# First block of a two-block transformer: low parts of weights on VectorE in the head norms and branches, head copies on ScalarE, wider rotation, six early gate units

## Chip, cores and metric

The kernel runs on one core of one Trainium2 chip. The metric is the device time of one execution in microseconds (us), the median of several runs. A core has TensorE (PE, matrix products; PEld is its weight load), VectorE (DVE), ScalarE (ACT), GpSimd (POOL) and SyncE (SP), whose queue issues the weight transfers here. Each engine runs its own queue in order.

## The reference, cut to what matters

256 tokens of width 1024 pass a first block and then two layers of a second block. Only the first block is touched. What it computes:

```python
h = rmsnorm(x, mix_norm_g)
proj = h @ w_in                       # 1024 x 5632
qa, ka, va, qd, kd, vd, qm, graw = split(proj)   # 3x384, 3x384, 256, 3x1024 columns
qa = rope(rmsnorm(heads(qa)), positions)         # 6 heads of 64; ka, qd, kd alike
qm = rmsnorm(heads(qm))                          # 4 heads
mkv = rmsnorm(mem) @ w_mem_kv                    # 1024 x 512
o_a = moba_attention(qa, ka, va) @ w_branch_moba
o_d = dilated_attention(qd, kd, vd) @ w_branch_dil
o_m = memory_attention(qm, rmsnorm(mk), mv) @ w_branch_mem
g = sigmoid(graw)                                # three gates of 1024 columns
x = x + (g0 * o_a + g1 * o_d + g2 * o_m) @ w_out
# then a feed-forward part with a convolution over three tokens, then the second block
```

All of it is in float32, which sets how the weights are handled.

## The kernel before, in words

**Split weights.** A weight slab of 128 rows is loaded by `wload` (L88) into `raw`; ScalarE rounds it into `hi` (L102) and another engine subtracts, `lw = raw - hi` (L103). The product is then three matmuls: `hi` and `lw` against the high part of the activations (L184, L185), `hi` against their low part (L187). Which engine makes `lw` follows a pattern set by `lo_on`: `lo_on(V, GP)` takes VectorE and GpSimd in turn, `lo_on(GP)` GpSimd alone. `raw` has four buffers, `hi` and `lw` three each, so the parts of a slab are made two to three slabs ahead of their use.

**Units.** `gemm_n` (L189) goes over the slabs of a product; with 1024 columns a slab is one unit of 12 matmuls of 128x512 (four accumulators in PSUM, of which there are four in all), with 512 columns six matmuls.

**Order of the first block.** The projection runs over column groups of 1024, 1024 and 512 (L363), then the memory projection of 512 columns (L371, eight units). Meanwhile VectorE and ScalarE run the head norms (`head_norm`, L407) and the rotation (`rope_pair`, L423) on the finished columns `pj`. `head_T` (L439) transposes q and k on TensorE and copies them into `qkT`, the middle group of three on VectorE (L451), the others on ScalarE (L449). The 24 gate units (3 gates by 8 slabs) are a list `fill`: `some_fill(2)` (L484) takes two ahead of the first `head_T`, `run_pairs` (L284) takes one after each of 16 attention steps, and what is left (six) runs at L508. The attention (L212) forms scores (L221), their maximum on VectorE (L236), the exponential on ScalarE (L243), transposes (L262), and the product with v (L275). Then come three branch products of 3, 3 and 2 slabs (L512); VectorE multiplies each by its gate (L518) and adds it to `merged` (L521, eight adds of 128x512). `merged` is transposed (L529) and multiplied by `w_out` (L533).

**What sets the order.** The kernel is written as straight code; a planner orders each engine's instructions by the place in the code (earlier is preferred) and by when it estimates operands and buffers to be ready. On the chip that order is fixed: an engine whose next instruction has to wait holds up everything behind it.

**GpSimd's part before.** In the memory projection every second `lw` is GpSimd's (L347, `lo_on(V, GP)`); from L481, `lo_on(GP)`, all 24 gate units, the 8 branch slabs and the 8 slabs of `w_out` are GpSimd's. From L537 on the two engines take turns again.

Of the kernel before, what the change touches and what calls it, by code (L numbers as in the profile page):

```python
# [10 lines left out]
F32 = mybir.dt.float32  # L11
# [39 lines left out]
def moba_peer_stack_kernel(ctx: ExitStack, tc: tile.TileContext, A, out):  # L51
    nc = tc.nc
    V, SC, GP, PE, SY = nc.vector, nc.scalar, nc.gpsimd, nc.tensor, nc.sync
# [14 lines left out]
    def tmp_tile():  # L68
        tmp = ptmp.tile([128, 512], F32)
        return tmp  # L70
# [7 lines left out]
    def P(name, i=None):  # L78
        o, w = PV[name]
        return pv[:, o:o + w] if i is None else pv[:, o + i:o + i + 1]  # L80
# [4 lines left out]
    def lo_on(*pat):  # L85
        pol["pat"], pol["i"] = pat, 0
# [19 lines left out]
    def split(hi, lo, ps, scale=None):  # L106
        if scale is None:
            SC.activation(hi, ps, AF.Copy)
            V.tensor_sub(lo, ps, hi.bitcast(F32))
        else:  # L110
            SC.activation(hi, ps, AF.Copy, scale=scale)  # L111
            V.scalar_tensor_tensor(lo, ps, scale, hi.bitcast(F32), op0=ALU.mult, op1=ALU.subtract)  # L112
# [39 lines left out]
    def norm_T(src, scratch, g, hi, lo):  # L152
        with tc.high_priority(offset=150):
            rstd, sq = row_rstd(src, scratch)
            for h in range(2):
                sl = slice(h * 512, (h + 1) * 512)
                asc = SC.activation(scratch[:, 0, sl], src[:, 0, sl], AF.Copy, scale=rstd[0])
                xs = V.tensor_scalar(scratch[:, 1, sl], src[:, 1, sl], rstd[1], None, op0=ALU.mult)
            hold["n"], hold["ins"] = 4, (asc.ins, xs.ins)
            for c in range(0, KC, 2):  # L160
                ps = tmp_tile()
                for t in range(2):
                    for c2 in range(2):
                        PE.transpose(ps[:, c2 * 256 + t * 128:c2 * 256 + (t + 1) * 128],
                                     scratch[:, t, (c + c2) * 128:(c + c2 + 1) * 128], ident)
                for c2 in range(2):
                    split(hi[:, c + c2, :], lo[:, c + c2, :], ps[:, c2 * 256:(c2 + 1) * 256],
                          scale=g[:, c + c2:c + c2 + 1])
# [20 lines left out]
    def gemm_n(units, ncols, ah, al, order=None, pre=()):  # L189
        nh = (ncols + 511) // 512  # L190
        accs = [acc_tile() for _ in range(2 * nh)]
        order = order or range(len(units))
        for i, c in enumerate(order):
            wh, wl = pre[i] if i < len(pre) else wload(units[c], ncols)
            gemm_n_unit(accs, wh, wl, ncols, ah, al, c, i == 0, i == len(units) - 1)
        return accs
# [87 lines left out]
    def run_pairs(gens, fill, per):  # L284
        live = list(gens)
        while live:
            for g in list(live):
                if next(g, live) is live:
                    live.remove(g)
            for _ in range(per):  # L290
                if fill:
                    fill.pop(0)()
# [21 lines left out]
    with ExitStack() as b1:  # L314
        ab = b1.enter_context(tc.tile_pool(name="b1", bufs=1))
        at = b1.enter_context(tc.tile_pool(name="b1at", bufs=2))
# [32 lines left out]
        pj = ab.tile([128, 2, 2560], F32)  # L349
        kv = ab.tile([128, 2, 512], F32)  # L350
        graw = ab.tile([128, 2, 3 * D], F32)
# [15 lines left out]

        mh = ab.tile([128, KC, S], F32R, name="mh", tag="mh")
        ml = ab.tile([128, KC, S], F32R, name="ml", tag="ml")
        norm_T(mem, xn, P("mem"), mh, ml)  # L370
        accs = gemm_n([A["w_mem_kv"][c * 128:(c + 1) * 128, :] for c in range(KC)], 512, mh, ml)  # L371
        evac_pj(accs, 0, 512, kv)

        with tc.issue_after(first_xs):
# [23 lines left out]
            tab = ab.tile([128, 4, 4, 2, 32], F32)  # L398
# [22 lines left out]
                V.tensor_mul(v, v, rs[:, t, :nheads, None].to_broadcast([128, nheads, 64]))  # L421

        def rope_pair(c0, ty0):  # L423
            for t in range(2):
                for i in range(2):
                    v = pj[:, t, c0 + i * 384:c0 + (i + 1) * 384].rearrange("p (h d) -> p h d", d=64)
                    x1, x2 = v[:, :, :32], v[:, :, 32:]
                    T = [tab[:, ty0 + i, k, t, None, :].to_broadcast([128, 6, 32]) for k in range(4)]
                    ta = at.tile([128, 6, 32], F32, name="ta")
                    tb = at.tile([128, 6, 32], F32, name="tb")  # L430
                    tcc = at.tile([128, 6, 32], F32, name="tcc")
                    V.tensor_mul(ta, x1, T[0])
                    V.tensor_mul(tb, x2, T[1])
                    V.tensor_mul(tcc, x1, T[2])
                    V.tensor_mul(x2, x2, T[3])
                    V.tensor_sub(x1, ta, tb)
                    V.tensor_add(x2, tcc, x2)

        def head_T(src, c0, w, s0):  # L439
            for c in range(0, w // 128, 2):  # L440
                n = min(2, w // 128 - c)
                ps = tmp_tile()
                for i in range(n):
                    for t in range(2):
                        PE.transpose(ps[:, i * 256 + t * 128:i * 256 + (t + 1) * 128],
                                     src[:, t, c0 + (c + i) * 128:c0 + (c + i + 1) * 128], ident)
                d = qkT[:, s0 + c:s0 + c + n, :].rearrange("p a b -> p (a b)")
                if (c // 2) % 2 == 0:
                    SC.copy(d, ps[:, :n * 256])  # L449
                else:  # L450
                    V.tensor_copy(d, ps[:, :n * 256])  # L451

        oh = ab.tile([128, KC, S], F32R, name="oh", tag="mh")
        ol = ab.tile([128, KC, S], F32R, name="ol", tag="ml")
# [1 line left out]
        def qkf(s0):  # L456
            return lambda h: qkT[(h % 2) * 64:(h % 2) * 64 + 64, s0 + h // 2, :]

        def vf(src, c0):
            return lambda h, k: src[:, k, c0 + h * 64:c0 + (h + 1) * 64]  # L460
# [16 lines left out]
        def some_fill(n):  # L477
            for _ in range(min(n, len(fill))):
                fill.pop(0)()

        lo_on(GP)  # L481
        head_norm(pj, 0, 12, "a")
        rope_pair(0, 0)
        some_fill(2)  # L484
        head_T(pj, 0, 768, 0)
        head_norm(pj, 1152, 12, "d")
        rope_pair(1152, 2)
        moba = [attention(at, (2 * hp, 2 * hp + 1), qkf(0), qkf(3), vf(pj, 768), False,
                          (oh[:, hp, :], ol[:, hp, :])) for hp in range(3)]
# [2 lines left out]
                         cmul=[ctab[:, 0, :128], ctab[:, 1, :]]) for hp in range(3)]  # L492
        mma = [attention(at, (2 * hp, 2 * hp + 1), qkf(12), qkf(14), vf(kv, 256), True,
                         (oh[:, 6 + hp, :], ol[:, 6 + hp, :])) for hp in range(2)]
        run_pairs(moba[:2], fill, 1)
        head_T(pj, 1152, 768, 6)
        head_norm(pj, 2304, 4, "q")
        head_norm(kv, 0, 4, "k")
        for src, c0, ty in ((pj, 2304, 4), (kv, 0, 5)):
            for t in range(2):  # L500
                v = src[:, t, c0:c0 + 256].rearrange("p (h d) -> p h d", d=64)
# [5 lines left out]
        run_pairs(mma, fill, 1)  # L507
        some_fill(len(fill))  # L508

        merged = xn  # L510
        for b, (k0, kn) in enumerate([(0, 3), (3, 3), (6, 2)]):
            accs = gemm_n([A["w_branch"][(k0 + c) * 128:(k0 + c + 1) * 128, :] for c in range(kn)],  # L512
                          1024, oh[:, k0:, :], ol[:, k0:, :])
            for t in range(2):
                for h in range(2):
                    g = graw[:, t, b * 1024 + h * 512:b * 1024 + (h + 1) * 512]
                    m = merged[:, t, h * 512:(h + 1) * 512]
                    V.scalar_tensor_tensor(m if b == 0 else g, g, 1.0, accs[t * 2 + h],  # L518
                                           op0=ALU.add, op1=ALU.mult)
                    if b:  # L520
                        V.tensor_add(m, m, g)  # L521
        half = ab.tile([128, 1], F32)
        V.memset(half, 0.5)
        uh, ul = hT_tiles()
        for c in range(0, KC, 2):
            ps = tmp_tile()
# [18 lines left out]
        for j in range(NF):  # L545
            ys = []
            for s in range(2):
                cc = s * NF + j
                wh, wl = wload(A["w_up"][2 * j + s], 1024)
                ps = tmp_tile()[:, :256]  # L550
# [39 lines left out]
    for l in range(L):  # L590
        with ExitStack() as mx:
            ab = mx.enter_context(tc.tile_pool(name=f"mx{l}", bufs=1))
            at = mx.enter_context(tc.tile_pool(name=f"mxat{l}", bufs=2))
# [54 lines left out]
            for k, bn in enumerate(("br", "bi")):  # L648
                ps = tmp_tile().rearrange("p (a t) -> p a t", a=2)
# [159 lines left out]
        with ExitStack() as pr:  # L809
# [31 lines left out]
            for h in range(8):  # L841
                ps = tmp_tile()
# [104 lines left out]
            for k in range(3):  # L947
                ps = tmp_tile()[:, :S]
                for t in range(2):
                    PE.transpose(ps[:, t * 128:(t + 1) * 128], ev[:, k, t], ident)  # L950
                ps = ps.rearrange("p (g b) -> p g b", b=2)
# [32 lines left out]
            for i in range(npair):  # L984
                n = NPRE + 2 * i
                u_pair(n, done * TG, (V, GP if i % 2 else V))
                want = min(ng, -(-ng * (i + 1) // (npair - 1)))
                while done < want:
                    g, oh = ready.pop(0)
# [8 lines left out]
            for n in range(NK):  # L998
                wh, wl = wload(A["v"][l, n], 1024, lo=V)
                vh, vl, c = (ah, al, n % 8) if n > 1 else (v0[:, :2], v0[:, 2:], n)  # L1000
# [4 lines left out]
    with ExitStack() as fin:  # L1005
        ab = fin.enter_context(tc.tile_pool(name="fin", bufs=1))
# [5 lines left out]
        for t in range(2):  # L1012
            for h in range(2):
                sl = slice(h * 512, (h + 1) * 512)
# [4 lines left out]
def layout(inputs):  # L1019
# [5 lines left out]
    a["mem"] = c(f["mem"][0])  # L1025
    a["positions"] = c(f["positions"][0].reshape(2, 128).T)

    def chunks(v, n):
        return v.reshape(n, 128).T

# [77 lines left out]
```

## Time and profile before

| | us |
|---|---|
| median of three runs (2447.13 to 2459.99) | 2455.22 |
| the profiled execution, its own time | 2449.0 |
| its span, first to last instruction | 2447.2 |
| PE busy | 2312.7 |
| DVE busy | 1601.4 |
| ACT busy | 1192.7 |
| POOL busy | 750.1 |
| the stretch from the head norms to the transposes for `w_out` | 40 to 256 |

How to read it: the profile lists each engine's instructions with start, duration and, for the idle time ahead of an instruction, what ended it. "Waits" sums that idle time by who waited for whom. A timeline row with xN merges N instructions in a row. The clock granted to TensorE is given as a share of full speed: 1.00 is 2.4 GHz, 0.50 is 1.2 GHz. Share of busy time counts an instruction from its start to its end, so an instruction that stands still inside its run counts as busy.

### The profile page before, as it was taken

The numbers are of one execution on the slowest core, as the hardware profiler recorded it, in microseconds if no ns is written. First come the engines' busy times: TensorE is split into PE (matmuls) and PEld (weight loads), VectorE is DVE, ScalarE is ACT, GpSimd is POOL, SyncE is SP. The second block draws the span as 40 slices with busy tenths as digits, with TensorE's granted clock in tenths as the row PEclk, the third lists the DMA queues.
The fourth block names the chain that finished last, engine by engine and source line by source line (L and its number), as shares of the span: only waits on it lengthen the run. The fifth ranks groups of instructions, "written<-read, shape, count | busy, mean of one in ns | idle before, by whom it ended". The sixth has DMA issues, their size and how long they took to land. (4 is left out here: it accounts for less than half of the span.)

```text
span 2447.2 us, 39099 instructions
## 1 busy us (share of the span) xinstructions
PE 2312.7 (95%) x15096; PEld 2078.0 (85%) x15096; DVE 1601.4 (65%) x3117; ACT 1192.7 (49%) x1837; POOL 750.1 (31%) x299
## 2 busy tenths in 40 slices
PE   7799899978998999999999997899899999999998
PEld 6577799877898999998888877689899999888886
DVE  8732566788487366776666668848736677666665
ACT  5444455533443554445555553344355444555553
POOL 2437344373579411110000006257941111000000
PEclk9899899997999999999999998899999999999999
DMA  5424355433454554555665553335455455555664
GB/s 201 133 83 151 127 179 184 156 114 100 131 165 153 173 163 157 165 165 188 196 191 195 192 170 107 101 130 165 155 173 163 157 164 164 190 196 191 195 192 146
DMA packets 111524, 392.89 MB, mean 161 GB/s; under 512 B 13272, under 2 KB 13912, under 8 KB 111080
## 3 DMA queue, kind: packets, MB, share of 16 engines
q1 hardware_dynamic: 108288, 384.42, 48.9%
q10 hardware_dynamic: 3048, 5.97, 0.7%
q8 instruction: 118, 1.93, 0.3%
q14 instruction: 70, 0.57, 0.1%
HBM read 389.28 MB, written 1.05 MB: 160 GB/s over the span
## 5 line engine op out<-in xcount | busy, mean ns | idle before, releaser
L103 POOL TENSOR_TENSOR lw<-raw,hi 128x1024 fp32r<-128x1024 f32 (+2 forms) x295 | 749.9, 2549 | 1332.7 <-ACT hi L102 737.3
L102 ACT ACTIVATE hi<-raw 128x1024 fp32r<-128x1024 f32 (+2 forms) x748 | 777.5, 1040 | 709.9 <-PE tmp L202 343.3
L203 PE MATMUL tmp<-thi,lw 128*128 128x256 f32 (+1 forms) x2832 | 805.7, 285 | 36.5 <-POOL lw L103 36.5
L201 PE MATMUL tmp<-thi,hi 128*128 128x256 f32 (+1 forms) x2832 | 813.6, 287 | 5.5 <-DVE tlo L112 2.8
L202 PE MATMUL tmp<-tlo,hi 128*128 128x256 f32 (+1 forms) x2832 | 804.1, 284 | 0.3
L103 DVE TENSOR_TENSOR lw<-raw,hi 128x1024 fp32r<-128x1024 f32 (+1 forms) x453 | 549.5, 1219 | 215.1 <-ACT hi L102 213.8
L203 PEld LDWEIGHTS tmp<-thi,lw 128*128 128x128 f32 (+1 forms) x2832 | 544.1, 192 | 40.2 <-POOL lw L103 39.7
L201 PEld LDWEIGHTS tmp<-thi,hi 128*128 128x128 f32 (+1 forms) x2832 | 544.5, 192 | 9.8 <-DVE tlo L112 4.8
L202 PEld LDWEIGHTS tmp<-tlo,hi 128*128 128x128 f32 (+1 forms) x2832 | 544.7, 192 | 2.2 <-DVE tlo L112 0.7
L185 PE MATMUL acc<-lw,thi 128*128 128x512 f32 x1248 | 489.5, 392 | 6.7 <-DVE lw L103 5.4
L184 PE MATMUL acc<-hi,thi 128*128 128x512 f32 x1248 | 489.4, 393 | 0.0
L187 PE MATMUL acc<-hi,tlo 128*128 128x512 f32 x1248 | 392.5, 391 | 0.0
L185 PEld LDWEIGHTS acc<-lw,thi 128*128 128x128 f32 x1248 | 235.2, 189 | 58.7 <-DVE lw L103 6.8
L184 PEld LDWEIGHTS acc<-hi,thi 128*128 128x128 f32 x1248 | 235.3, 189 | 49.8 <-DVE pj L361 0.6
L187 PEld LDWEIGHTS acc<-hi,tlo 128*128 128x128 f32 x1248 | 234.9, 188 | 49.0 <-DVE tlo L112 0.3
L111 ACT ACTIVATE thi<-W 128x256 fp32r<-128x256 f32 x252 | 104.4, 419 | 284.6 <-PE acc L185 284.6
L961 DVE TENSOR_TENSOR oh<-iotab,eT 128x1024 f16<-128x1024 f16 x128 | 85.0, 691 | 164.0 <-PE acc L973 164.0
L112 DVE SCALAR_TENSOR_TENSOR tlo<-W,thi 128x256 fp32r<-128x256 f32 x252 | 106.0, 425 | 111.3 <-PE acc L187 111.3
L965 DVE TENSOR_TENSOR oh<-oh,gT 128x1024 f16<-128x1024 f16 x128 | 87.3, 683 | 0.0
L978 ACT COPY W<-acc 128x344 f32<-128x344 f32 (+42 forms) x128 | 38.7, 303 | 84.3 <-DVE W L976 84.3
L675 DVE SCALAR_TENSOR_TENSOR yc<-yp,pv,yc 128x256 f32<-128x256 f32 x120 | 73.9, 655 | 0.0
L973 PE MATMUL acc<-oh 128*128 128x128 f16 x1024 | 73.8, 219 | 0.0
(321 smaller groups left out, 2053.0 us busy)
## 6 DMA issues: line engine op xcount, KB each, us to landing
raw<-in_u_dram SPq DMA_DIRECT2D x256, 512.0 KB, 3.6
raw<-in_v_dram SPq DMA_DIRECT2D x256, 512.0 KB, 3.6
raw<-in_w_up_dram SPq DMA_DIRECT2D x44, 512.0 KB, 3.6
raw<-in_w_in_dram SPq DMA_DIRECT2D x40, 512.0 KB, 3.6
raw<-in_w2t_dram SPq DMA_DIRECT2D x32, 512.0 KB, 4.2
raw<-in_wq_dram SPq DMA_DIRECT2D x32, 512.0 KB, 3.6
raw<-in_w_out_dram SPq DMA_DIRECT2D x24, 512.0 KB, 3.6
raw<-in_w_down_dram SPq DMA_DIRECT2D x22, 512.0 KB, 3.6
```

Source lines behind the costliest of these rows:

```text
L102: SC.activation(hi[:, :ncols], r, AF.Copy)
L103: lo.tensor_sub(lw[:, :ncols], r, hi[:, :ncols].bitcast(F32))
L111: SC.activation(hi, ps, AF.Copy, scale=scale)
L112: V.scalar_tensor_tensor(lo, ps, scale, hi.bitcast(F32), op0=ALU.mult, op1=ALU.subtract)
L184: PE.matmul(ps, lh, wh[:, sl], start=first, stop=False)
L185: PE.matmul(ps, lh, wl[:, sl], start=False, stop=False)
L187: PE.matmul(ps, ll, wh[:, sl], start=False, stop=last)
L201: PE.matmul(ps, wh[:, sl], ah[:, c, :], start=(c == 0), stop=False)
L202: PE.matmul(ps, wh[:, sl], al[:, c, :], start=False, stop=False)
L203: PE.matmul(ps, wl[:, sl], ah[:, c, :], start=False, stop=(c == KC - 1))
L961: V.tensor_tensor(oh[:, 0].rearrange("p g j n b -> p (g j) n b"), iotab[:, None].to_broadcast([128, TG, 128, 2]), eT[:, g].rearrange("p g ...
L965: V.tensor_mul(oh[:, 1], oh[:, 0, :, 1, None].to_broadcast([128, TG // 2, 2, 128, 2]), gT[:, g, :, None].to_broadcast([128, TG // 2, 2, 12 ...
```

## The change

Five edits, all in the first block:

1. `lo_on(V)` ahead of the memory norm: all eight memory slabs' `lw` on VectorE (before: in turn). `lo_on(V)` in place of `lo_on(GP)` ahead of the head norms, and `lo_on(V, GP)` ahead of the first `run_pairs`; `lo_on(V)` ahead of the branches, which holds for `w_out` too.
2. `rope_pair` works on both token halves at once: 12 instructions of 128x384 in place of 24 of 128x192.
3. `head_T` copies on ScalarE alone.
4. `some_fill(6)` in place of `some_fill(2)`.
5. The branch adds work on both token halves: four of 128x1024 behind all four gate products of their branch, in place of eight of 128x512 between them.

```diff
         mh = ab.tile([128, KC, S], F32R, name="mh", tag="mh")
         ml = ab.tile([128, KC, S], F32R, name="ml", tag="ml")
+        lo_on(V)
         norm_T(mem, xn, P("mem"), mh, ml)
...
         def rope_pair(c0, ty0):
-            for t in range(2):
-                for i in range(2):
-                    v = pj[:, t, c0 + i * 384:c0 + (i + 1) * 384].rearrange("p (h d) -> p h d", d=64)
-                    x1, x2 = v[:, :, :32], v[:, :, 32:]
-                    T = [tab[:, ty0 + i, k, t, None, :].to_broadcast([128, 6, 32]) for k in range(4)]
...
+            for i in range(2):
+                v = pj[:, :, c0 + i * 384:c0 + (i + 1) * 384].rearrange("p t (h d) -> p t h d", d=64)
+                x1, x2 = v[:, :, :, :32], v[:, :, :, 32:]
+                T = [tab[:, ty0 + i, k, :, None, :].to_broadcast([128, 2, 6, 32]) for k in range(4)]
...
                 d = qkT[:, s0 + c:s0 + c + n, :].rearrange("p a b -> p (a b)")
-                if (c // 2) % 2 == 0:
-                    SC.copy(d, ps[:, :n * 256])
-                else:
-                    V.tensor_copy(d, ps[:, :n * 256])
+                SC.copy(d, ps[:, :n * 256])
...
-        lo_on(GP)
+        lo_on(V)
         head_norm(pj, 0, 12, "a")
         rope_pair(0, 0)
-        some_fill(2)
+        some_fill(6)
         head_T(pj, 0, 768, 0)
...
+        lo_on(V, GP)
         run_pairs(moba[:2], fill, 1)
...
         run_pairs(mma, fill, 1)
         some_fill(len(fill))
 
+        lo_on(V)
         merged = xn
...
                     V.scalar_tensor_tensor(m if b == 0 else g, g, 1.0, accs[t * 2 + h],
                                            op0=ALU.add, op1=ALU.mult)
-                    if b:
-                        V.tensor_add(m, m, g)
+            if b:
+                for h in range(2):
+                    sl = slice(b * 1024 + h * 512, b * 1024 + (h + 1) * 512)
+                    m = merged[:, :, h * 512:(h + 1) * 512]
+                    V.tensor_add(m, m, graw[:, :, sl])
```

## Rows read from the trace of the kernel before

**Rows 1.** The page: busy us, share of the span and instructions of each engine.

```profile
PE 2312.7 (95%) x15096; PEld 2078.0 (85%) x15096; DVE 1601.4 (65%) x3117; ACT 1192.7 (49%) x1837; POOL 750.1 (31%) x299
```

**Rows 2.** What PE waited for, 40 to 125: total, times, longest (us).

```profile
PE tmp L221 <- DVE qkT L451: 8.7, 1, 8.7
PE acc L185 <- POOL lw L103: 4.7, 2, 4.1
PE acc L185 <- DVE lw L103: 4.1, 3, 1.9
```

**Rows 3.** What PE waited for, 205 to 280.

```profile
PE tmp L529 <- DVE xn L521: 3.4, 3, 2.7
PE acc L184 <- DVE graw L518: 3.2, 1, 3.2
```

**Rows 4.** Stretches: length, then busy of PE, PEld, DVE, ACT, POOL, clock, DMA.

```profile
41.00:106.00 65.00, 56.20 (x236) 43.85 (x234) 57.06 (x118) 29.91 (x46) 31.27 (x16) 0.92 0.46 141
87.05:92.34 5.29, 5.29 (x12) 4.14 (x13) 2.04 (x6) 0.82 (x2) 1.18 (x1) 0.50 0.70 208
114.70:126.70 12.00, 12.00 (x31) 7.09 (x32) 2.91 (x11) 3.46 (x11) 0.00 (x0) 0.51 0.01 1
147.10:150.50 3.40, 3.40 (x9) 2.34 (x9) 2.05 (x10) 1.68 (x8) 0.00 (x0) 0.51 0.01 2
164.90:170.50 5.60, 5.60 (x26) 3.12 (x25) 2.02 (x9) 2.41 (x5) 2.87 (x2) 1.00 0.44 129
246.50:249.10 2.60, 2.60 (x7) 1.97 (x6) 0.77 (x2) 1.06 (x1) 1.10 (x1) 0.50 0.00 0
```

**Rows 5.** Timeline, memory projection: start, duration, engine, line; idle before, releaser.

```profile
81.13 7.10 POOL L103 TENSOR_TENSOR lw<-raw,hi 128x512 fp32r<-128x512 f32 x2 [3.26 <-ACT hi L102]
82.54 0.40 PE L184 MATMUL acc<-hi,mh 128*128 128x512 f32 x1
83.04 0.68 DVE L103 TENSOR_TENSOR lw<-raw,hi 128x512 fp32r<-128x512 f32 x1
```

**Rows 6.** Timeline, first gate units to the first scores.

```profile
96.26 11.74 POOL L103 TENSOR_TENSOR lw<-raw,hi 128x1024 fp32r<-128x1024 f32 x5 [2.11 <-ACT hi L102]
98.73 2.32 DVE L122 TENSOR_TENSOR rs_th<-hrs 128x24 f32<-128x24 f32 x1
104.04 1.25 PE L445 MATMUL tmp<-ident,pj 128*128 128x128 f32 x10
105.25 1.06 ACT L449 COPY qkT<-tmp 128x512 f32<-128x512 f32 x2
111.20 0.18 DVE L122 TENSOR_TENSOR rs_th<-hrs 128x24 f32<-128x24 f32 x1
113.86 0.68 DVE L451 COPY qkT<-tmp 128x512 f32<-128x512 f32 x1
```

**Rows 7.** Timeline: PE's late memory units, and transposes ahead of later scores.

```profile
78.48 0.50 PE L185 MATMUL acc<-lw,thi 128*128 128x512 f32 x1 [1.16 <-DVE lw L103]
139.94 1.91 PE L445 MATMUL tmp<-ident,pj 128*128 128x128 f32 x16
```

**Rows 8.** Timeline, DVE: a late low part, and the branches' products and adds.

```profile
76.66 1.76 DVE L103 TENSOR_TENSOR lw<-raw,hi 128x512 fp32r<-128x512 f32 x1
229.43 2.79 DVE L518 SCALAR_TENSOR_TENSOR xn<-graw,acc 128x512 f32<-128x512 f32 x4 [23.65 <-PE acc L187]
239.14 4.89 DVE L521 TENSOR_TENSOR xn<-xn,graw 128x512 f32<-128x512 f32 x2
245.15 1.28 DVE L521 TENSOR_TENSOR xn<-xn,graw 128x512 f32<-128x512 f32 x2
```

**Rows 9.** DVE's groups by form, 40 to 120: busy us, mean ns.

```profile
L103 DVE TENSOR_TENSOR lw<-raw,hi 128x1024 fp32r<-128x1024 f32 x3 | 3.6, 1213 | 0.0
...
L433 DVE TENSOR_TENSOR tb<-pj,tab 128x192 f32<-128x192 f32 x8 | 2.8, 346 | 0.0
```

**Rows 10.** Timeline, ACT at the gate units left for the end: one unit's beat.

```profile
212.30 1.06 ACT L102 ACTIVATE hi<-raw 128x1024 fp32r<-128x1024 f32 x1 [1.66 <-PE acc L187]
```

More of the change, by code (lines that the diff above doesn't have):

```diff
@@ L423, in rope_pair @@
         def rope_pair(c0, ty0):
-            for t in range(2):
-                for i in range(2):
-                    v = pj[:, t, c0 + i * 384:c0 + (i + 1) * 384].rearrange("p (h d) -> p h d", d=64)
-                    x1, x2 = v[:, :, :32], v[:, :, 32:]
-                    T = [tab[:, ty0 + i, k, t, None, :].to_broadcast([128, 6, 32]) for k in range(4)]
[L429 to L437, printed above, removed]
+            for i in range(2):
+                v = pj[:, :, c0 + i * 384:c0 + (i + 1) * 384].rearrange("p t (h d) -> p t h d", d=64)
+                x1, x2 = v[:, :, :, :32], v[:, :, :, 32:]
+                T = [tab[:, ty0 + i, k, :, None, :].to_broadcast([128, 2, 6, 32]) for k in range(4)]
+                ta = ab.tile([128, 2, 6, 32], F32, name="ta")
+                tb = ab.tile([128, 2, 6, 32], F32, name="tb")
+                tcc = ab.tile([128, 2, 6, 32], F32, name="tcc")
+                V.tensor_mul(ta, x1, T[0])
+                V.tensor_mul(tb, x2, T[1])
+                V.tensor_mul(tcc, x1, T[2])
+                V.tensor_mul(x2, x2, T[3])
+                V.tensor_sub(x1, ta, tb)
+                V.tensor_add(x2, tcc, x2)
         def head_T(src, c0, w, s0):
```

## The prediction

> **What bounds the kernel now.** I read the page first: PE is busy for 2312.7 us, 95% of the span, and no other engine is above 65% [rows 1]. So an edit pays only where PE stands still or runs slowly, and the next view is what PE waited for in the stretch that the diff touches. Five groups of waits matter between 40 and 256 us. Ahead of the attention they are 8.7 us for `qkT` (one wait), 4.7 us for GpSimd's `lw` (one of 4.1, one of 0.6) and 4.1 us for VectorE's `lw` (three) [rows 2]. In the branches they are 3.2 us for an accumulator that a gate product should have freed, and 3.4 us for the adds into `merged` [rows 3].
>
> The third view is the clock in the stretches behind these waits. After the 4.1 us wait, PE runs 12 matmuls in 5.29 us at a granted clock of 0.50, which is 1.2 GHz; behind the 8.7 us wait the clock is 0.51 for 12.0 us; behind the 3.2 us wait 0.50 for 2.60 us [rows 4]. So each long wait is paid for twice.
>
> The last view is the timelines of VectorE and GpSimd beside the waits. A norm instruction of 128x24 lasts 2.32 us while GpSimd runs five `lw` in 11.74 us without a gap; the same instruction lasts 0.18 us when GpSimd is idle [rows 6]. The two-input instructions of the two engines take turns here. It also goes the other way: GpSimd needs 7.10 us for two `lw` of 128x512 while VectorE rotates the heads [rows 5].
>
> **Part 1: VectorE makes the memory `lw`.** PE stands still behind a matmul that starts at 82.54 [rows 5]. This wait of 4.1 us goes if `lw` comes from VectorE: there the same slab takes 0.68 us, in the same rotation [rows 5]. What is late next is the slab's `hi`, which is ready earlier. The 12 slow matmuls go back to PE's full rate. That rate follows from one gate unit: a beat is 1.06 + 1.66 = 2.72 us [rows 10] for 12 matmuls, 0.227 each. So 5.29 - 2.72 = 2.6 us are regained, and the term is 4.1 + 2.6 = **6.7 us**. The smaller wait for GpSimd at the first gate unit goes too: **0.6 us**. And PE's wait of 1.16 us for VectorE [rows 7] came from an `lw` of 1.76 us [rows 8], 1.08 more than the same form takes elsewhere, beside GpSimd's first memory slab, which moves to VectorE: **1.1 us**. The other two waits for VectorE (2.9 us) lie earlier than the edit, and I leave them.
>
> **Parts 3 and 4: `qkT` and six units.** The scores waited from 106.0 to 114.7 us for the one copy on VectorE's queue, at 113.86, behind the norms of the memory heads; ScalarE had copied its two groups from 105.25 on, in 1.06 us [rows 6]. With the third copy on ScalarE, it costs ScalarE about 0.5 us, and ScalarE is idle there. In addition four more units, 4 x 2.72 = 10.9 us of PE work, stand ahead of the scores, more than the hole is long. I take the wait of 8.7 us as gone, but for 1.0 us between the transposes and the last copy (bounds 0, if a unit fits in between, and 4.7, if the norms still hold something up): **7.7 us**. The four units are missing from the end, where six ran one after the other at PE's full rate [rows 10]; two are left, the 16 attention steps keep one unit each, and the branches start with heads finished long before. So no cover is lost there: 0 us.
>
> The clock: 12.0 us at 0.51 [rows 4] hold the scores of two pairs and seven gate matmuls. At full clock such scores take 5.6 us [rows 4], seven matmuls 1.6, so 4.8 us could come back. But transposes and scores in one run are not safe: from 139.94 on, transposes [rows 7] were followed by scores, and at 147.1 us, without a gap, the clock fell to 0.51 for 3.4 us [rows 4]. I expect one such stretch at the first scores, half of 3.4 = 1.7 lost, so **3.1 us** (bounds 0 and 4.8).
>
> **Part 5 and the branch `lw`.** In the second branch two adds took 4.89 us, between gate products, while GpSimd made `lw`; two others took 1.28 us [rows 8]. PE waited 3.2 us for the products behind them [rows 3]. The four products of the first branch, which has no adds, ran in 2.79 us [rows 8], and PE didn't wait there. Now the adds come behind the products, and nothing of GpSimd's runs. The wait goes, with its 2.60 us at half clock (six intervals, at full clock 6 x 0.227 = 1.4): 3.2 + 1.2 = **4.4 us**. At the end of the third branch, PE waited 3.4 us in all [rows 3]. After the change the chain is one product, 0.7 us, and an add of 128x1024, by the nearest row of that size 1.21 us [rows 9], then transposes of the first half and a rest of about 0.3 us for the second: 2.2 us. **1.2 us** gained (bounds -1.2, if an `lw` is put in between, and 2.0).
>
> **Part 2: the rotation.** 24 x 0.346 = 8.3 us become 12 instructions of double length; by interpolating between 192 elements (0.346) and 1024 (1.213) [rows 9] one takes 0.55, together 6.6 us. PE doesn't wait for the rotation itself, so this is 0 us on the path and 1.7 us of slack for VectorE, twice. If the wider form were slower by half, it would cost the same 3 us of slack.
>
> **What it adds.** VectorE's queue gets 4 more memory `lw` (0.68 each), 6 gate `lw` (1.21) ahead of the scores, 9 among the 18 others, and 16 in the branches and `w_out`. With four of the memory slabs that it had, 39 `lw` stand in its queue. Behind each stand norms, maxima and copies. Before, 3 of VectorE's 11 `lw` between 40 and 120 us came late, by 1.4 us on average (4.1 us [rows 2]); one of the three was GpSimd's doing. I take 3 late ones of about 1.0 us: **-3 us**. The lower bound of the cost is 0, the upper the old rate, 39 x 3/11 x 1.4 = 15 us.
>
> **Sum.** 6.7 + 0.6 + 1.1 + 7.7 + 3.1 + 4.4 + 1.2 - 3 = 21.8, rounded to 22 us. The profiled execution took 2449.0 us, 1.8 more than its span, so that one would become 2427. It lies 6.2 us below the median of the runs, 2455.2; against the median I forecast **2433 us**.
>
> **The rivals.** *A: the units or copies don't get ahead.* The planner orders PE by estimates that don't contain the taking of turns seen above. If it puts the transposes and scores ahead of the added units, or if the scores wait for something else in VectorE's queue, the 7.7 and 3.1 stay lost: 21.8 - 10.8 = 11, or 2444 us. Against it: the six units stand earlier in the code and need only weights, and GpSimd's slow `lw`, which made the third unit late, is gone. Here the change would do only half of what it says. Chance 0.18.
>
> *B: VectorE becomes the bound (slower).* VectorE was busy for 57.06 of 65 us from 41 to 106 us [rows 4], and ten new `lw` are 4 x 0.68 + 6 x 1.21 = 10.0 us: 67 in 65. If those 57 us are real work, each `lw` comes behind one instruction too many; at 1.16 us [rows 7] for each of 39 that is 45 us against a gain of 24.8: 2475 us. It is slower than before from 22 late ones on, and by more than 0.5% from 32 on. Against it: part of the 57 us is standing still, as 2.32 us for an instruction of 0.18 [rows 6], and the new scheme removes it. Chance 0.06.
>
> The Trainium skill speaks for B: its page Perfetto Trace Analysis (Optimizing Scalar/DVE Operations) says that work of a saturated DVE may well be offloaded to other engines, even to GPSIMD, and this change does the reverse. The same sentence group adds that offloading between those two might not help, as they share a read port. By the first half the time would be that of B; the trace so far bears out the second half more.
>
> **How the numbers follow.** Forecast 0.76, A 0.18, B 0.06. Within the forecast the known ends are: all new `lw` in time and the clock high, 24.8 + 1.7 + 1.0 + 0.8 = 28.3 us gained; or `lw` late at the old rate, 21.8 - 12 = 10 us gained. Runs of the same kernel lie within 13 us (2447 to 2460), so 6 to either side. The range goes from 2420 (28.3 and the spread) to 2448 (A and the spread's larger part); B lies outside. About 0.5%, 12 us, is what a measurement of this kernel can tell from no change. Faster by more than that, below 2443: 0.74, the forecast without its slowest end. Within it: 0.20, A and that end. Slower: 0.06.
>
> **What would show it.** Right: no wait of PE for GpSimd's `lw` between 75 and 100 us; norm instructions of 128x24 at 0.18 us throughout; PE's hole ahead of the first scores below 2 us, with six units ahead of them, and scores at a clock near 1.00; products of the second branch in 2.8 us without adds between; no wait of PE for an accumulator there. Wrong: new waits of PE for VectorE's `lw`, more than five of them between 75 and 130 us (B); scores still behind a hole of over 4 us (A); the clock at 0.50 for over 5 us at the first scores; or a change after 282 us, where the code is the same, of more than 5 us.

## The result and the profile after

The changed kernel takes 2422.48 us in the median of four runs (2420.75 to 2425.97), the kernel before 2456.56 in four (the three above and one more): a ratio of 0.9875, 95% interval 0.9851 to 0.9899. The ratio isn't the quotient of the two medians, which would be 0.9861. The forecast was 2433, with 2420 to 2448 as its range. The profiled execution took 2423.2 us, its span is 2421.5. One execution of all that follow, of the kernel with the low parts alone, took 2839.79 us at a mean granted clock of 0.74 (0.97 in its others) and is left out below.

The wider rotation also takes its three intermediates from a pool with one buffer each, where they had two; the diff above doesn't show that line.

First, what PE waited for between 40 and 125 us in the changed kernel: total, times, longest. It answers to [rows 2].

```profile
PE acc L184 <- ACT pj L359: 1.6, 1, 1.6
PE acc L185 <- POOL lw L103: 1.3, 1, 1.3
PE acc L185 <- DVE lw L103: 1.1, 1, 1.1
```

The 8.7 us for `qkT` and the 4.7 us for GpSimd's memory and first gate parts are gone. What is left lies in the projection, which the change leaves alone: the 1.3 us for GpSimd end at 39.7 us, at the edge, the 1.6 at 65.1, and the 1.1 us for VectorE at 71.47. From the memory slabs to 125 us PE waits for no low part. Of the branch waits in [rows 3] this is left, between 205 and 280 us:

```profile
PE tmp L531 <- DVE xn L523: 2.0, 1, 2.0
```

The timeline of PE from the memory slabs to the first scores (start, duration, engine, line), first row of each group:

```profile
78.31 0.40 PE L184 MATMUL acc<-hi,mh 128*128 128x512 f32 x1
...
89.86 0.40 PE L184 MATMUL acc<-hi,thi 128*128 128x512 f32 x1
...
106.69 1.25 PE L445 MATMUL tmp<-ident,pj 128*128 128x128 f32 x10
...
109.02 0.48 PE L221 MATMUL tmp<-qkT 64*128 64x128 f32 x2
```

A norm instruction of 128x24 beside them:

```profile
92.63 0.18 DVE L122 TENSOR_TENSOR rs_th<-hrs 128x24 f32<-128x24 f32 x1
```

There is no hole any more: 77 gate matmuls stand between 89.86 and 109.02, five of them between the transposes and the scores, while ScalarE copies. The stretches (length, busy of PE, PEld, DVE, ACT, POOL, clock, DMA) show the clock:

```profile
41.00:106.00 65.00, 62.19 (x275) 48.73 (x273) 58.73 (x126) 31.82 (x46) 12.12 (x8) 1.00 0.58 178
109.00:114.40 5.40, 5.40 (x26) 3.11 (x25) 2.23 (x8) 2.02 (x4) 0.00 (x0) 1.00 0.57 184
136.00:146.00 10.00, 10.00 (x39) 7.54 (x39) 3.59 (x16) 3.52 (x10) 2.05 (x1) 0.69 0.01 2
```

The scores that took 9.0 us at 1.2 GHz take 5.4 at 2.4 GHz. PE is busy for 62.19 of the 65 us where it had 56.20 [rows 4]; VectorE, with more to do, for 58.73 where it had 57.06. The third row lies in the second scores: from about 136 us the clock falls without a gap in PE's work, as it did at 147.1 us in the kernel before [rows 4]. That the first scores run at 2.4 GHz throughout is in part luck. The kernel with one gate unit moved behind them (under More of the same) has the same code up to there, and its profiled execution has half clock in its first scores:

```profile
112.00:119.00 7.00, 7.00 (x19) 4.47 (x19) 1.84 (x8) 3.46 (x11) 0.00 (x0) 0.51 0.05 21
```

In the branches, VectorE's queue now reads:

```profile
222.31 1.88 DVE L517 SCALAR_TENSOR_TENSOR graw<-graw,acc 128x512 f32<-128x512 f32 x3
224.11 2.35 DVE L523 TENSOR_TENSOR xn<-xn,graw 128x1024 f32<-128x1024 f32 x2
```

Products first, then two wide adds in 2.35 us, where [rows 8] had 4.89 for two narrow ones.

### The profile page after: what moved, and what is told of

It is laid out like the page before. It is cut to its first block, busy times and chain, and to the rows that moved or that the text cites. A ratio compares the mean times of both kernels' runs of the same rounds, so it can differ in the third digit from the quotient of the medians.

```text
span 2421.5 us, 39065 instructions
## 1 busy us (share of the span) xinstructions
PE 2306.6 (95%) x15096; PEld 2072.7 (86%) x15096; DVE 1613.1 (67%) x3122; ACT 1193.3 (49%) x1839; POOL 668.3 (28%) x264
## 5 line engine op out<-in xcount | busy, mean ns | idle before, releaser
L103 POOL TENSOR_TENSOR lw<-raw,hi 128x1024 fp32r<-128x1024 f32 (+2 forms) x260 | 668.1, 2577 | 1389.8 <-ACT hi L102 777.2
L103 DVE TENSOR_TENSOR lw<-raw,hi 128x1024 fp32r<-128x1024 f32 (+1 forms) x488 | 589.3, 1213 | 234.5 <-ACT hi L102 233.2
```

Of the source, the lines that this page charges most:

```text
L103: lo.tensor_sub(lw[:, :ncols], r, hi[:, :ncols].bitcast(F32))
```

## The experiments

### The kernel before once more

> The kernel before once more, unchanged, for a second profiled execution and its spread (2447 to 2460 us so far, the profiled one at 2449). Theory (the spread comes from GpSimd and VectorE taking turns in an order that differs between executions, mostly in the first block): the two profiled executions differ by several us up to 282 us and by under 2 us behind it, if their times differ. Rival: the difference lies in the second block, whose code the change doesn't touch.

Measured: ten runs from 2445.24 to 2459.03 us, median 2454.95. In the same turn 25 further runs of the kernel before, against which the ratios of this turn are taken, have a median of 2447.12: 13 lie from 2445 to 2448, 12 from 2451 to 2460. So the executions come in two groups here, and the median falls into the one that has more runs. The ratio of the ten to the 25 is 1.0014 (0.9997 to 1.0030). In the two later turns the kernel before has medians of 2454.43 and 2453.30, in seven runs each.

The second profiled execution has a span of 2455.5 us, 8.3 more than the first. These are stretches of the first execution, from the first scores to the first branch product and from there to the feed-forward norm:

```profile
282.20:2447.20 2165.00, 2071.73 (x13988) 1889.06 (x13988) 1448.39 (x2717) 1065.66 (x1619) 623.23 (x241) 0.97 0.51 164
222.90:282.20 59.30, 48.74 (x209) 38.45 (x207) 27.02 (x52) 20.74 (x28) 34.57 (x15) 0.95 0.45 140
114.70:222.90 108.20, 107.15 (x541) 83.61 (x542) 29.80 (x101) 49.85 (x105) 49.02 (x21) 0.93 0.30 94
```

and the same stretches of the second:

```profile
114.40:227.10 112.70, 111.65 (x541) 86.26 (x542) 29.77 (x101) 49.89 (x105) 49.04 (x21) 0.89 0.31 90
227.10:290.40 63.30, 51.10 (x209) 40.62 (x207) 28.57 (x52) 20.91 (x28) 34.55 (x15) 0.91 0.41 132
290.40:2455.50 2165.10, 2073.14 (x13988) 1890.23 (x13988) 1446.68 (x2717) 1065.51 (x1619) 626.84 (x241) 0.97 0.52 163
```

The rest of the program takes the same time. The 8.2 us lie in the attention (4.5, the same 541 matmuls at 0.89 instead of 0.93) and in the branches (4.0); up to the first scores the second is 0.3 faster. In the branches PE is busy for 2.4 us more with the same 209 matmuls, at 0.91 instead of 0.95, and the other 1.6 us are longer waits for the adds, 5.0 us in place of 3.4 [rows 3]: there the turns fall otherwise. Two adds of the third branch, first execution and then second:

```profile
249.62 1.91 DVE L521 TENSOR_TENSOR xn<-xn,graw 128x512 f32<-128x512 f32 x2
```

```profile
253.84 4.83 DVE L521 TENSOR_TENSOR xn<-xn,graw 128x512 f32<-128x512 f32 x2
```

So the theory holds in half: the place is the first block, and one part, 1.6 us, is turns falling otherwise; the larger part, 6.9 us, is more time at 1.2 GHz. What decides between the two is open.

### One edit alone, from the kernel before

**The copies on ScalarE.**

```diff
-                if (c // 2) % 2 == 0:
-                    SC.copy(d, ps[:, :n * 256])
-                else:
-                    V.tensor_copy(d, ps[:, :n * 256])
+                SC.copy(d, ps[:, :n * 256])
```

> The kernel before with one edit alone: the head copies all on ScalarE. Theory (the scores waited for one copy that stood in VectorE's queue behind the memory heads' norms): the hole of 8.7 us ahead of the first scores shrinks to under 2 us, and part of the half clock behind it goes: 7 us plus 3 to 5, so 10 to 12 us less than before. Rival (the hole needs more PE work ahead of it, the copy only names the wait): the hole stays above 6 us, 0 to 3 us less.

Measured: 2447.01 us (2442.38 to 2448.60) in ten runs, ratio 0.9984 to the 25 runs, interval 0.9969 to 0.9999. PE's longest waits from 40 to 125 us:

```profile
PE acc L185 <- POOL lw L103: 5.1, 3, 3.2
PE acc L184 <- ACT pj L359: 2.3, 1, 2.3
PE acc L185 <- DVE lw L103: 2.0, 2, 1.6
```

The hole is gone, with scores from 106.69 on instead of 114.68, yet only 0 to 8 us of the time. The first branch product comes at 216.70 us instead of 222.94; of the hole's 8.0 us, 6.2 are still there. Then the branches take 63.2 us, as in the second execution of the kernel before, not 59.3 as in the first. Held against that second execution the branches are equal and the first branch product comes 10.4 us earlier, so that the span is 10.1 us shorter, the theory's 10 to 12; held against the first it is 1.8. The theory on the hole holds. What the copy alone is worth depends on the execution that it is held against, and the runs say 0 to 8.

**Six units.**

```diff
-        some_fill(2)
+        some_fill(6)
```

> The kernel before with one edit alone: six gate units ahead of the first head transposes, their low parts still on GpSimd. Theory (any 9 us of ready work fills the hole): four units are 10.9 us, the hole goes below 1 us, with the clock behind it: 10 to 13 us less than before; GpSimd needs 2.4 us for a unit's low part against 2.72 for its matmuls, so it keeps up. Rival (GpSimd and the norms take turns, so the units come late too): PE waits for GpSimd's low parts by 2 us or more, and at most 6 us are gained.

Measured: 2455.12 us (2443.78 to 2456.97), ratio 1.0017 to the 25 runs, interval 1.0000 to 1.0034, where the unchanged kernel has 1.0014: nothing gained. The theory falls. PE's wait, and VectorE and GpSimd at that time:

```profile
121.79 0.76 PE L221 MATMUL tmp<-qkT 64*128 64x128 f32 x2 [6.03 <-DVE qkT L451]
```

```profile
95.36 14.38 POOL L103 TENSOR_TENSOR lw<-raw,hi 128x1024 fp32r<-128x1024 f32 x6 [2.04 <-ACT hi L102]
109.98 5.16 POOL L103 TENSOR_TENSOR lw<-raw,hi 128x1024 fp32r<-128x1024 f32 x2 [0.24 <-ACT hi L102]
```

```profile
97.83 2.33 DVE L122 TENSOR_TENSOR rs_th<-hrs 128x24 f32<-128x24 f32 x1
...
104.91 5.10 DVE L421 TENSOR_TENSOR pj<-pj,hrs 128x256 f32<-128x256 f32 x2
109.94 2.95 DVE L502 TENSOR_TENSOR pj<-pj,rowv 128x256 f32<-128x256 f32 x2
...
120.96 0.68 DVE L451 COPY qkT<-tmp 128x512 f32<-128x512 f32 x1
```

The rival named the link but the wrong victim. GpSimd's parts come in time for the units. But beside each added part one more instruction of the norms takes 1.6 to 2.6 us, so the norms end later, and the copy behind them moves from 113.86 to 120.96. The work that should fill the hole pushes its end away: 6.0 us are left of 8.7.

**The low parts' engines**, all four changes of `lo_on`, in two turns; the profile is of the second.

> The kernel before with one edit alone: all four changes of which engine makes the low parts (memory, gates, branches); old rotation, old copies, two units, old adds. Theory: the memory wait with its clock (6.7), the two small waits (1.7) and most of the branch waits (3 to 5) go; the hole ahead of the scores stays, at 5 to 9 us, since PE comes there about as much earlier as the norms end earlier: 11 to 14 us less than before in all. Rival (the hole came from the norms being slowed): the hole falls below 2 us and about 22 us are gained.

> The low parts' engines alone once more (the kernel before with those four changes), for a profile. Its times were 20 us below the kernel before, near the rival's 22. If the slowed norms were the cause of the hole, the hole ahead of the first scores is below 2 us with two units and VectorE's copy; if not, it is 5 us or more and the gain lies elsewhere. In the branches, with the old order of adds but VectorE's low parts, PE's wait for an accumulator is below 1.5 us if turns with GpSimd made it, and above 2.5 us if the order of the adds did.

Measured: 2427.84 to 2432.21 us in four runs, median 2429.37, ratio 0.9923 (0.9904 to 0.9942); the second time 2427.18 (2426.51 to 2427.85), ratio 0.9892 (0.9860 to 0.9924). This one edit carries most of the gain. The waits of PE from 40 to 125 us:

```profile
PE acc L185 <- DVE lw L103: 3.3, 3, 1.9
PE tmp L221 <- DVE qkT L452: 3.2, 1, 3.2
```

The hole is 3.2 us, between theory and rival, and its rest has the rival's cause too: GpSimd makes one gate part from 95.25 to 97.64 us, and a norm instruction behind it takes 2.18 us.

```profile
95.25 2.39 POOL L103 TENSOR_TENSOR lw<-raw,hi 128x1024 fp32r<-128x1024 f32 x1 [20.04 <-ACT hi L102]
95.48 2.18 DVE L119 TENSOR_SCALAR hrs<-hrs 128x24 int32<-128x24 int32 x1
```

In the branches there is no wait for an accumulator, in spite of the old order of the adds: the turns made that wait, not the order. The wait ahead of the transposes for `w_out` is shorter with the old adds than with the wide ones, 1.3 us against 2.0:

```profile
PE tmp L532 <- DVE xn L524: 1.3, 1, 1.3
```

### One edit undone, from the changed kernel

The diffs: no `lo_on(V)` ahead of the memory norm; `lo_on(GP)` for all gate units; `some_fill(2)`; the middle copy on VectorE; `lo_on(GP)` ahead of the branches.

> The changed kernel with one part undone: the memory slabs' low parts on VectorE and GpSimd in turn again. Theory (GpSimd can't get its turn while VectorE rotates the heads): a wait of PE for GpSimd of 3 to 5 us comes back between 78 and 90 us, with a stretch at half clock: 5 to 8 us slower than the changed kernel. Rival (GpSimd's part is only slower by its own 0.6 us, and two slabs of lead hide that): within 1 us.

> The changed kernel with one part undone: all gate units' low parts on GpSimd. Theory: the norms of the memory heads take 2.3 us an instruction again beside GpSimd, but nothing on PE's path waits for them, as the copies are ScalarE's and six units lie ahead: 0 to 3 us slower than the changed kernel, PE's hole ahead of the scores below 2 us. Rival (the slowed norms were the cause of the hole): 6 us or more slower.

> The changed kernel with one part undone: two gate units ahead of the head transposes. Theory (copies on ScalarE alone already remove the hole): the hole is below 2 us, 0 to 3 us slower than the changed kernel. Rival (the units fill the hole): a hole of 5 us or more with half clock behind it, 8 to 12 us slower.

> The changed kernel with one part undone: the middle head copy on VectorE again. Theory (the norms are done by 104 us, ahead of the transposes at 106.7): the copy runs at once, the hole is below 1.5 us, 0 to 2 us slower than the changed kernel. Rival (whatever stands on VectorE waits behind the norms and low parts): a hole of 3 us or more, 4 to 8 us slower.

> The changed kernel with one part undone: the low parts of the branches and of w_out on GpSimd again; the adds stay wide and behind the products. Theory (turns with GpSimd lengthen an add, the order keeps it off PE's path in the second branch): no wait of PE for an accumulator, 1 to 3 us more ahead of the transposes for w_out; 1 to 3 us slower than the changed kernel from the first branch product to the feed-forward norm. Rival (GpSimd's part is the whole cause): 4 us or more slower there.

The medians stand beside 2422.48 us of the changed kernel, which ran in another turn; the ratios are to the kernel before in the same turn. All five intervals overlap with that of the changed kernel, so the times alone show no part to be needed, and what follows rests on the stages of one profiled execution each. They come from PE's timeline: the memory slabs from their first matmul to the first gate matmul, and what PE lost from there to the first scores, which is the length less 0.227 us for each gate matmul between (77; 29 with the six units undone, 74 with the copies undone, 27 in the kernel before) and 1.0 for the transposes.

| undone | median us | ratio to before, interval | memory slabs us | lost ahead of the scores us |
|---|---|---|---|---|
| nothing | 2422.48 | 0.9875 (0.9851 to 0.9899) | 11.55 | 0.7 |
| memory `lw` | 2425.27 | 0.9894 (0.9863 to 0.9926) | 14.82 | 0.2 |
| gate `lw` | 2424.98 | 0.9897 (0.9864 to 0.9931) | 11.55 | 1.8 |
| six units | 2422.35 | 0.9879 (0.9847 to 0.9910) | 11.56 | 1.4 |
| copies | 2422.58 | 0.9885 (0.9851 to 0.9919) | 11.54 | 1.1 |
| branch `lw` | 2427.22 | 0.9892 (0.9862 to 0.9922) | 11.54 | 0.6 |
| kernel before | 2456.56 | | 17.99 | 9.8 |

The memory slabs cost 3.3 us more with turns, and the 1.16 us wait just ahead of them is back; together that is less than the 5 to 8 us of the theory, and the wait in the slabs is for VectorE's part, not for GpSimd: a rotation instruction of 0.55 us takes 1.63 beside a GpSimd part, and the `lw` that PE wants stands behind it.

```profile
83.36 1.63 DVE L431 TENSOR_TENSOR ta<-pj,tab 128x384 f32<-128x384 f32 x1
84.92 0.68 DVE L103 TENSOR_TENSOR lw<-raw,hi 128x512 fp32r<-128x512 f32 x1
```

The gate parts, the units and the copy follow their theories: none of them is needed once the others are there. With GpSimd's gate parts a norm instruction takes 2.33 us again, and PE doesn't wait for the norms; it waits for GpSimd's first part:

```profile
PE acc L185 <- POOL lw L103: 1.3, 1, 1.3
```

The branch parts cost most: from the first branch product to the feed-forward norm it is 57.55 us against 54.04, 3.5 more where the theory had 1 to 3. It comes by one wait ahead of the transposes for `w_out`, 2.0 us in the changed kernel; the row and its cause, the wide adds at twice their 2.35 us:

```profile
PE tmp L531 <- DVE xn L523: 5.4, 1, 5.4
```

```profile
223.26 4.62 DVE L523 TENSOR_TENSOR xn<-xn,graw 128x1024 f32<-128x1024 f32 x2
```

No wait for an accumulator there, as the theory had it: the order of the adds protects PE from the turns, and an engine without turns needs no such order.

### More of the same

```diff
         head_T(kv, 0, 256, 14)
+        some_fill(1)
         run_pairs([moba[2], dil[0]], fill, 1)
```

> The changed kernel with one gate unit between the second group of head transposes and the scores behind it. In the changed kernel TensorE went on at 1.2 GHz from about 135 to 142 us, in the scores that follow 20 transposes without a gate matmul between. Theory (that run of transposes and scores lets the clock fall): with 12 gate matmuls between them no stretch at half clock there, 2 to 4 us less up to the branches. Rival (the clock falls there for another reason, or falls elsewhere instead): the half-clock time between 100 and 200 us stays within 3 us of that of the changed kernel, and the time too.

Measured: 2422.62 us (2420.55 to 2423.44), ratio 0.9875 (0.9850 to 0.9899). The stretch from 100 to 200 us, changed kernel and then this one:

```profile
100.00:200.00 100.00, 98.97 (x512) 76.70 (x511) 42.53 (x119) 46.51 (x103) 20.75 (x9) 0.93 0.32 101
```

```profile
100.00:200.00 100.00, 98.94 (x518) 77.17 (x517) 43.54 (x116) 47.54 (x104) 21.37 (x9) 0.95 0.34 106
```

The clock is hardly higher, and the time is the same, as the rival said. The fall in the second scores is gone, but this execution has one in the first scores, the row shown under the result. Whether the gate unit moved the fall or the fall moves by itself, one execution can't tell.

```diff
         SC.dma_start(mem, A["mem"].rearrange("(t p) d -> p t d", p=128))
-        lo_on(V, GP)
+        lo_on(V)
...
-        lo_on(V, GP)
+        lo_on(V)
         run_pairs(moba[:2], fill, 1)
```

> The changed kernel with more of the same: every low part of the first block up to the feed-forward part on VectorE, the projection's and the attention's too. Theory (turns between the two engines are the loss, VectorE has room): the waits of PE for low parts up to 125 us (2.4 us in the changed kernel) shrink, 0 to 3 us faster. Rival (VectorE, busy 58.7 of 65 us there, is the bound when it gets about a dozen more): PE's waits for VectorE's low parts grow by 3 us or more, 3 to 8 us slower.

Measured: 2416.41 us (2415.20 to 2420.09), ratio 0.9850 (0.9824 to 0.9876), 6 us below the changed kernel, where the theory had 0 to 3. The first of the two edits holds for the projection, the second for the attention. The two intervals overlap, but on the same chip in the same turn the kernel with the gate unit, at the changed kernel's time, had its lowest at 2420.55, above all four runs of this one. Its one wait of PE between 40 and 125 us, and its busy times:

```profile
PE acc L185 <- DVE lw L103: 0.3, 1, 0.3
```

```profile
41.00:106.00 65.00, 64.50 (x294) 51.11 (x293) 59.85 (x136) 34.74 (x50) 0.00 (x0) 1.00 0.59 182
```

PE works for 64.50 of 65 us. VectorE took over all of GpSimd's low parts here and is busy for 1.1 us more than in the changed kernel, in a stretch in which PE does 294 matmuls in place of 275: what it gained in work it lost in standing still. VectorE isn't the bound. The first scores come at 103.18 us in place of 109.02, so the 6 us lie ahead of them.

## Why the prediction was right, step by step

| term | forecast us | profiled executions us |
|---|---|---|
| up to the first memory matmul | 1.1 | 79.74 to 78.31: 1.4 |
| memory slabs with their clock | 6.7 | 17.99 to 11.55: 6.4 |
| hole and first gate wait | 7.7 + 0.6 | lost 9.8 to 0.7: 9.1 |
| clock, scores to first branch | 3.1 | 0.2 |
| branches and `w_out` | 4.4 + 1.2 | 59.3 to 54.0: 5.3 |
| `lw` late on VectorE | -3 | included above |
| behind the feed-forward norm | 0 | 2165.0 to 2161.7: 3.3 |
| sum | 21.8, rounded to 22 | 25.7 |

The first three rows and the branches agree within 1 us each, and the norm instructions are at 0.18 us, the products without adds between, as foretold. The wait of 1.16 us in the first row is of the projection's third group (it multiplies `thi`), though the caption of [rows 7] says memory; it is gone here and back with the memory parts undone. The "clock" row is net of the gate units that moved ahead: 108.26 us with 21.75 units left became 96.67 with 17.58, at 2.72 us a unit. Against the second execution of the kernel before it would be 4.7. The forecast expected one stretch at half clock behind the first scores; it came behind the second, and one more from about 160 us, so the 3.6 us gained at the first scores were given back.

**Where the sum had luck.** Two terms failed and cancel: the cost of 3 us for late low parts did not come, and 2.9 of the 3.1 us of clock did not come either. The stages that the forecast speaks of gained 22.4 us between the two profiled executions, where it said 21.8; the other 3.3 lie in code that it left at 0.

**The -3 us for late low parts** was the step that failed. Low parts on VectorE weren't late: of PE's 4.1 us of waits for them [rows 2], 2.9 lay ahead of the edit and 1.16 is gone, and behind the edit no new one came. The rate of three late in eleven had been taken beside GpSimd's turns, and not one of the three but all seem to be their doing: with GpSimd out of the projection too, 0.3 us of the 4.1 are left. Rival B's reading of 57 us of busy time as work fell with it, by the kernel with all low parts on VectorE.

**Units and copies.** The forecast booked 7.7 us for edits 3 and 4, with the reason that ready work fills a hole. Alone, the units gain nothing, and the copies remove the hole. With the low parts moved, either of the two can be left out. The low parts alone, booked elsewhere, cut the hole from 8.7 to 3.2 us. So the terms of the sum weren't independent.

**The adds.** The forecast booked 4.4 us for the wide adds and the branch parts together, with the order of the adds as one reason. The order wasn't needed once VectorE made the low parts.

**The 2433.** It was 2455.2 less 22. The profiled execution of the kernel before was 6 us faster than its median, and that distance was carried over. The changed kernel's profiled execution lies at its median, so the measured gain between medians is 34 us. 8 of the 12 us too few are this step (the medians lie 34.1 us apart, the profiled executions 25.7). The second execution of the kernel before loses more to turns and to half clock than the one that was read. Which of the two is typical isn't fixed: the 25 runs have their median at 2447.12, the first four at 2456.56.

The Trainium skill, in SBUF — State Buffer (Who interferes with whom), says that a VectorE instruction with two SBUF inputs contends with a GpSimd instruction that reads SBUF, and that the port pair which they share is an exclusive lock. The 2.33 us of a 0.18 us instruction and the 4.62 us of adds that take 2.35 agree. The 2.18 us instruction above reads one tile only, and this sentence doesn't speak of it. The Trainium skill, in Perfetto Trace Analysis (Optimizing Scalar/DVE Operations), which the prediction held against the change, says that offloading some work of a saturated VectorE, even to GpSimd, may make sense. The 59.85 us with 0.3 us of waiting show that VectorE wasn't saturated here, as its busy share counts the standing still.

**Open.** The wider rotation and the wide adds were neither run alone nor undone. The low parts alone leave 5 to 7 us to the changed kernel; as the units and the copies undone cost nothing, these two edits may hold them, or the half clock that falls otherwise from one execution to the next. Nor does a run tell why turns cost the memory slabs 6.4 us in the kernel before and 3.3 in the changed one. Why the same code behind the feed-forward norm took 3.3 us less, and why the kernel before has executions of 2446 and of 2456 us, wasn't settled. Of the 3.3 us, 2.3 arise in one place, from 1182 to 1294 us behind that norm, and 1.0 behind the last matmul. From that norm on the program takes 2160.9 to 2161.8 us in the changed kernel, in the one with all low parts on VectorE and in those with the low parts alone, with the memory parts, the units or the branch parts undone, or with the gate unit added, and 2164.2 to 2166.8 in the five others, the kernel before in both executions among them; I found nothing in the edits that separates the two groups.

## What to carry to other kernels

Where two engines take turns, read a short instruction's duration beside its usual one before taking a busy share for load: work taken back from the slower engine can cost the faster one next to nothing, here 1.1 us. Test parts that aim at the same hole alone as well, as work put in to fill a hole can delay what the hole waits for. Profile the kernel before more than once, and take the gain against the spread of its executions, not against the one that the profile happened to catch.

## What the runs showed of the hardware

TensorE's clock fell to 1.2 GHz without a gap in its work, in float32 scores that followed 20 transposes, in the kernel before (147.1 us, granted clock 0.51) and in the changed one (about 136 us, 0.69 over ten us). And moving the projection's low parts to VectorE as well raised its busy time from 58.73 to 59.85 us of 65, though GpSimd's 12.12 us went to nothing.
